# A second PSUM bank for the gates' matmuls, one bank fewer for the rest, and seven one-hot buffers in a one-core decoder block

## The chip, the cores and the metric

The kernel runs on one core of a Trainium2 chip. The metric is the device time of the program in microseconds (us). The core has engines that run side by side, each through its own queue in order: TensorE (PE, with its weight loads PEld), VectorE (DVE), ScalarE (ACT), GpSimd (POOL) and SyncE (SP, which here only issues transfers). The 16 DMA engines move the data. Matmuls write to PSUM, which has eight banks of 2 KiB per partition; ScalarE and VectorE empty it.

## What is computed

One decoder block on 1024 tokens of width 1024, in float32. Its first half is a mixer (sliding-window attention with sinks on 8 heads, and a short gated convolution, behind one input and before one output projection) with a residual and a layer norm. Its second half picks experts: for each token and each of 8 heads, 16 of 16384 single-neuron experts are chosen by two half keys, and their outputs are added up.

```python
h = layer_norm(DN_ALPHA * x + mix, ln1_g, ln1_b)
q = (h @ w_pq).reshape(T, 8, 256)
s1, s2 = q[..., :128] @ sub_keys1.T, q[..., 128:] @ sub_keys2.T
v1, i1 = top_k(s1, 16); v2, i2 = top_k(s2, 16)
cand = v1[..., :, None] + v2[..., None, :]
sc, pos = top_k(cand.reshape(T, 8, 256), 16)
e = i1[pos // 16] * 128 + i2[pos % 16];  g = softmax(sc)
a = gelu(einsum('tkd,td->tk', u_experts[e], h))
ff = einsum('tk,tkd->td', g * a, v_experts[e])
out = layer_norm(DN_ALPHA * h + ff, ln2_g, ln2_b)
```

## The kernel before

The tokens are eight blocks of 128. Three and a half of them (blocks 0, 6, 7 and half of block 1) are done by gathering rows: for each of the 128 chosen experts, GpSimd issues one indirect transfer that fetches a 1024-wide row of `u` (line 170) and later of `v` (line 183) for every token, and VectorE makes one pass over it (lines 172 and 185). The other four and a half blocks, 576 tokens, are done densely: every expert is computed for every token on TensorE, and a table of gates says which counts.

**Stage 1** (lines 211 to 683) goes through four groups of two blocks. For each group `project` multiplies 42 chunks of weights (line 399, eight matmuls a chunk): attention (`scores`, `values`), convolution (`conv`), output projection (`mixed`), norm (`normed`), and 16 chunks of expert queries with their key scores and searches (`keys_of`, lines 225 to 229 by `topk16`). While group g+1 is projected, a generator `side` works off what group g left: `product_keys` searches the candidates and decodes the chosen indices (lines 311 to 372), and for dense blocks `gates_of_all` builds the gate table. It takes eight tokens at a time: VectorE makes three one-hot tiles (`o1` in line 285, `oh` and `ol` in line 290; tag `hot`, four buffers for all three and for `f3`), TensorE multiplies them into a bank `pk` of four tokens (lines 296 and 297), and ScalarE empties the bank in two halves into the staging tiles `st` (line 300). After four such steps, one chunk of 32 tokens, SyncE stores both `st` tiles to the table `gd` in HBM (line 304); `st` has two buffers, so one set. There are 72 steps and 18 chunks. All other PSUM work of stage 1 uses `pm` (the projections, two banks) and `pt` (transposes, scores, the attention's `po`, all under the tag `tp`, three banks); the row passes hold two banks (`pg`). The gathered rows are put between the projections by `advance_rows`.

**Stage 2** (from line 686) reuses the SBUF space of stage 1. It loads the normed activations back (`hr`, split into `hT` on ScalarE and VectorE, lines 693 to 697), then runs 128 steps `up` (line 715) and 128 steps `down` (line 751) of 48 matmuls each, reading the gate table by `gq` (line 719). VectorE splits weights (`ul`, line 125), multiplies by gates (line 723), adds up (line 759), and makes the remaining row passes between.

What sets the order: the program is written in one stream, and a scheduler places its instructions engine by engine by its own timeline of the program, with the number of buffers and banks as limits. So a change of buffer counts can move instructions anywhere.

Of the kernel before, what the change touches and what calls it, by code (L numbers as in the profile page):

```python
# [13 lines left out]
F32 = mybir.dt.float32  # L14
F32R = mybir.dt.float32r
F16 = mybir.dt.float16
# [6 lines left out]
PS = bass.MemoryType.PSUM  # L23
DR = bass.MemoryType.DRAM

P = 128
# [27 lines left out]
OT = 8  # L54
# [25 lines left out]
def block_kernel(ctx: ExitStack, tc: tile.TileContext, d, out):  # L80
# [131 lines left out]
    with ExitStack() as s1:  # L212
        pa = s1.enter_context(tc.tile_pool(name="pa", bufs=1))
        gb = s1.enter_context(tc.tile_pool(name="gb", bufs=1))
        p1 = s1.enter_context(tc.tile_pool(name="p1", bufs=1))
        p2 = s1.enter_context(tc.tile_pool(name="p2", bufs=1))
        pk = s1.enter_context(tc.tile_pool(name="pk", bufs=1, space=PS))
        pm = s1.enter_context(tc.tile_pool(name="pm", bufs=2, space=PS))
        pt = s1.enter_context(tc.tile_pool(name="pt", bufs=3, space=PS))

        bias = p1.tile([P, 26], F32, name="bias")
        nc.sync.dma_start(bias, d["bias"])
# [14 lines left out]
        def gates_of_all(tb, e1, e2, g, first=0):  # L237


            f3 = gb.tile([P, 3, P], F32, name="f3", tag="hot", bufs=4)  # L240
            ei = gb.tile([P, P], I32, name="ei")
            V.tensor_copy(f3[:, 0], e1.rearrange("p h k -> p (h k)"))
            V.tensor_copy(ei, e2.rearrange("p h k -> p (h k)"))
            V.tensor_scalar(ei, ei, 7, None, op0=ALU.bitwise_and)
            V.tensor_copy(f3[:, 2], ei)
            V.tensor_tensor(f3[:, 1], e2.rearrange("p h k -> p (h k)"), f3[:, 2], op=ALU.subtract)
            tp = pk.tile([P, 4, P], F32, name="pk")
            for i in range(3):
                nc.tensor.transpose(tp[:, i], f3[:, i], ident)
            nc.tensor.transpose(tp[:, 3], g.rearrange("p h k -> p (h k)"), ident)  # L250
            iT = gb.tile([P, 5, P], F16, name="iT", bufs=2)
            act(iT[:, 0:3], tp[:, 0:3], AF.Copy)
            act(iT[:, 3], tp[:, 3], AF.Copy, scale=GSCALE)
            V.scalar_tensor_tensor(iT[:, 4], tp[:, 3], GSCALE, iT[:, 3], op0=ALU.mult, op1=ALU.subtract)
            i1w = gb.tile([P, P, OT], F16, name="i1w")
            act(i1w, tp[:, 0, :, None].to_broadcast([P, P, OT]), AF.Copy)

            def wide(o, i, n, step, t0):
                wshp = [P, n, HB // OT, OT]
                V.tensor_tensor(o.rearrange("p n (a t) -> p n a t", t=OT),  # L260
                                iT[:, i, t0:t0 + HB].rearrange("p (a t) -> p a t", t=OT)[:, None].to_broadcast(wshp),
                                keys[:, 0:n * step:step, None, :].to_broadcast(wshp), op=ALU.is_equal)

            shp = [P, P, OT]
            shr = [P, OT, P // OT, OT]
            for t0 in range(first, P, TG):
                if t0 % HB == 0:
                    da = gb.tile([P, 16, HB], F16, name="da")
                    wide(da, 1, 16, 8, t0)
                    db = gb.tile([P, 3, 8, HB], F16, name="db")  # L270
                    wide(db[:, 0], 2, 8, 1, t0)
                    for i in (1, 2):
                        V.tensor_tensor(db[:, i], db[:, 0], iT[:, 2 + i, None, t0:t0 + HB].to_broadcast([P, 8, HB]),
                                        op=ALU.mult)
                st = [gb.tile([P, NC // 2, TG], F32, name="st", bufs=2) for _ in range(2)]
                for t1 in range(t0, t0 + TG, OT):
                    ts = slice(t1, t1 + OT)
                    td = slice(t1 % HB, t1 % HB + OT)

                    def mk(name):  # L280
                        return gb.tile(shp, F16, name=name, tag="hot", bufs=4)

                    o1 = gb.tile([P, OT, P], F16, name="o1", tag="hot", bufs=4)
                    oh, ol = mk("oh"), mk("ol")
                    V.tensor_tensor(o1.rearrange("p t (a b) -> p t a b", b=OT),  # L285
                                    i1w[:, ts, None, :].to_broadcast(shr),
                                    row.rearrange("p (a b) -> p a b", b=OT)[:, None].to_broadcast(shr),
                                    op=ALU.is_equal)
                    for o, i in ((oh, 1), (ol, 2)):
                        V.tensor_tensor(o.rearrange("p (a b) t -> p a b t", b=8),  # L290
                                        da[:, :, None, td].to_broadcast([P, 16, 8, OT]),
                                        db[:, i, None, :, td].to_broadcast([P, 16, 8, OT]), op=ALU.mult)
                    for t2 in range(0, OT, 4):
                        ps = pk.tile([P, 4, P], F32, name="pk")
                        for t in range(4):
                            nc.tensor.matmul(ps[:, t], oh[:, :, t2 + t], o1[:, t2 + t], start=True, stop=False)  # L296
                            nc.tensor.matmul(ps[:, t], ol[:, :, t2 + t], o1[:, t2 + t], start=False, stop=True)
                        tt = t1 - t0 + t2
                        for z in range(2):
                            act(st[z][:, :, tt:tt + 4].rearrange("p n t -> p t n"),  # L300
                                ps[:, :, z * 64:(z + 1) * 64], AF.Copy, scale=1.0 / GSCALE)
                        yield
                for z in range(2):
                    nc.sync.dma_start(gd[(tb * P + t0 - DT0) // TG, :, z * 64:(z + 1) * 64], st[z])

        def product_keys(tb, v16, i16):
# [67 lines left out]
            if tb not in ROWS or tb == SHARED:  # L374
                yield from gates_of_all(tb, e1, e2, g, HALF if tb == SHARED else 0)
# [482 lines left out]
```

## Time and profile before

| | us |
|---|---|
| median of 3 runs | 2876.57 (2875.49 to 2882.86) |
| the profiled execution | 2877.42 |
| its span, first to last instruction | 2875.7 |
| TensorE busy | 2533.8 (88%) |
| VectorE busy | 2217.7 (77%) |
| GpSimd / ScalarE busy | 1286.0 / 845.0 |

Shares of busy time are means over both stages, which have different limits, so the stages are read apart: by slices, by stretches, and by what each engine waited for. The granted clock of TensorE has two levels here, 2.4 GHz (1.00 in the profile) and 1.2 GHz (0.50). Durations of neighbouring instructions can overlap a little, since one starts while the last one drains.

### The profile page before, as it was taken

The numbers are of one execution on the slowest core, as the hardware profiler recorded it, in microseconds if no ns is written. First come the engines' busy times: TensorE is split into PE (matmuls) and PEld (weight loads), VectorE is DVE, ScalarE is ACT, GpSimd is POOL, SyncE is SP. The second block draws the span as 40 slices with busy tenths as digits, with TensorE's granted clock in tenths as the row PEclk, the third lists the DMA queues.
The fourth block names the chain that finished last, engine by engine and source line by source line (L and its number), as shares of the span: only waits on it lengthen the run. The fifth ranks groups of instructions, "written<-read, shape, count | busy, mean of one in ns | idle before, by whom it ended". The sixth has DMA issues, their size and how long they took to land.

```text
span 2875.7 us, 45661 instructions
## 1 busy us (share of the span) xinstructions
PE 2533.8 (88%) x17220; PEld 2399.3 (83%) x17220; DVE 2217.7 (77%) x5055; ACT 845.0 (29%) x1486; POOL 1286.0 (45%) x1110
## 2 busy tenths in 40 slices
PE   9998899799868322199999999999999999999997
PEld 7887787678657222199999999999999999999997
DVE  2259999999999999678888888888888888632335
ACT  2213232232443333242222322232222222322322
POOL 0001533543433345356756666666666666312121
PEclk9899899799879555599999999999999999999998
DMA  6346999999888787989999999999999999633322
GB/s 206 98 157 213 358 359 343 335 345 328 302 309 304 264 303 269 333 273 360 335 331 347 337 334 329 333 337 342 334 331 334 332 331 337 232 115 104 108 88 74
DMA packets 285597, 805.36 MB, mean 280 GB/s; under 512 B 24992, under 2 KB 105152, under 8 KB 280640
## 3 DMA queue, kind: packets, MB, share of 16 engines
q0 software_dynamic: 132160, 481.39, 46.1%
q1 hardware_dynamic: 153216, 321.06, 32.8%
q8 instruction: 135, 2.21, 0.3%
q14 instruction: 86, 0.70, 0.1%
HBM read 753.56 MB, written 48.50 MB: 279 GB/s over the span
## 4 chain that ended last, share of the span: by engine, by line
PE 58%; DVE 12%; DMA 5%; issue 3%; POOL 1%; ACT 1%; POOLq 0%; DVEq 0%; ACTq 0%
PE pd L751 28%; PE pd L715 28%; DVE pg L185 2%; PE mm L399 2%; DVE row L172 2%; DMA row<-in_v,ix 2%; DMA gd<-st 1%; DMA row<-in_u,ix 1%; DVE ol L290 1%; DVE o L285 1%; DVE oh L290 1%; DMA uraw<-in_uT 1%; DVE scr L227 1%; ACT st L300 0%; DVE i L229 0%
## 5 line engine op out<-in xcount | busy, mean ns | idle before, releaser
L715 PE MATMUL pd<-hT,uh 128*128 128x288 f32 x4096 | 710.9, 296 | 46.6 <-ACT uh L124 46.6
L183 POOL DMA_INDIRECT row<-in_v,ix x448 | 495.2, 1105 | 487.9 <-DVE pg L185 240.5
L170 POOL DMA_INDIRECT row<-in_u,ix x448 | 462.6, 1032 | 542.7 <-DVE row L172 214.5
L715 PEld LDWEIGHTS pd<-hT,uh 128*128 128x128 f32 x4096 | 602.6, 189 | 46.8 <-ACT uh L124 46.8
L185 DVE SCALAR_TENSOR_TENSOR pg<-row,a,pg 128x1024 f32<-128x1024 f32 x448 | 574.2, 1282 | 29.9 <-DMA row<-in_v,ix 25.5
L172 DVE SCALAR_TENSOR_TENSOR row<-row,pg 128x1024 f32<-128x1024 f32 x448 | 536.3, 1213 | 30.3 <-DMA row<-in_u,ix 24.9
L125 POOL TENSOR_TENSOR vl<-vraw,vh 128x1024 fp32r<-128x1024 f32 x128 | 307.3, 2401 | 350.2 <-ACT vh L124 346.7
L751 PE MATMUL pd<-Wl,vh 128*128 128x288 f32 x2048 | 442.8, 295 | 0.0
L751 PE MATMUL pd<-Wh,vl 128*128 128x288 f32 x2048 | 442.3, 295 | 0.6 <-POOL vl L125 0.6
L751 PE MATMUL pd<-Wh,vh 128*128 128x288 f32 x2048 | 441.4, 295 | 0.7 <-DVE accT L759 0.7
L715 PE MATMUL pd<-hT,ul 128*128 128x288 f32 x2048 | 437.9, 295 | 0.0
L759 DVE TENSOR_TENSOR accT<-accT,pd 128x288 f32<-128x288 f32 x496 | 203.5, 450 | 216.5 <-PE pd L751 211.6
L751 PEld LDWEIGHTS pd<-Wh,vl 128*128 128x128 f32 x2048 | 330.9, 188 | 0.8 <-POOL vl L125 0.8
L751 PEld LDWEIGHTS pd<-Wh,vh 128*128 128x128 f32 x2048 | 330.5, 188 | 1.1 <-issue 0.9
L751 PEld LDWEIGHTS pd<-Wl,vh 128*128 128x128 f32 x2048 | 331.1, 188 | 0.1
L715 PEld LDWEIGHTS pd<-hT,ul 128*128 128x128 f32 x2048 | 329.8, 189 | 0.3 <-DVE ul L125 0.3
L124 ACT ACTIVATE vh<-vraw 128x1024 fp32r<-128x1024 f32 x128 | 135.8, 1061 | 537.1 <-PE pd L751 455.1
L125 DVE TENSOR_TENSOR ul<-uraw,uh 128x1024 fp32r<-128x1024 f32 x128 | 159.2, 1244 | 173.9 <-ACT uh L124 166.5
L296 PE MATMUL pk<-o,oh 128*128 128x128 f16 x576 | 116.7, 267 | 182.7 <-DVE oh L290 89.8
L399 PE MATMUL mm<-x,raw 128*128 128x256 f32 x1152 | 267.8, 384 | 7.9 <-DMA x<-in_xT 7.0
L399 PEld LDWEIGHTS mm<-x,raw 128*128 128x128 f32 x1152 | 213.6, 192 | 39.2 <-DMA raw<-in_wall 6.0
L124 ACT ACTIVATE uh<-uraw 128x1024 fp32r<-128x1024 f32 x128 | 135.8, 1061 | 370.4 <-PE pd L715 319.8
(218 smaller groups left out, 2977.5 us busy)
## 6 DMA issues: line engine op xcount, KB each, us to landing
raw<-in_wall SPq DMA_DIRECT2D x168, 512.0 KB
uraw<-in_uT SPq DMA_DIRECT2D x128, 512.0 KB
vraw<-in_vL SPq DMA_DIRECT2D x128, 512.0 KB
gd<-st SPq DMA_DIRECT2D x36, 1024.0 KB
gq<-gd SPq DMA_DIRECT2D x32, 1152.0 KB
row<-in_u,ix POOLq DMA_INDIRECT x448
row<-in_v,ix POOLq DMA_INDIRECT x448
x<-in_xT SPq DMA_DIRECT2D x16, 256.0 KB
```

The source lines that it names most:

```text
L124: act(dh, src, AF.Copy)
L125: eng.tensor_tensor(dl, src, dh.bitcast(F32), op=ALU.subtract)
L170: G.indirect_dma_start(out=row, out_offset=None, in_=d["u"], in_offset=bass.IndirectOffsetOnAxis(ap=ix[:, k:k + 1], axis=0))
L172: V.scalar_tensor_tensor(row, row, 1.0, h1p, op0=ALU.mult, op1=ALU.mult, accum_out=a[:, k:k + 1])
L183: G.indirect_dma_start(out=row, out_offset=None, in_=d["v"], in_offset=bass.IndirectOffsetOnAxis(ap=ix[:, k:k + 1], axis=0))
L185: V.scalar_tensor_tensor(acc, row, a[:, k:k + 1], acc, op0=ALU.mult, op1=ALU.add)
L290: V.tensor_tensor(o.rearrange("p (a b) t -> p a b t", b=8), da[:, :, None, td].to_broadcast([P, 16, 8, OT]), db[:, i, None, :, td].to_broa ...
L296: nc.tensor.matmul(ps[:, t], oh[:, :, t2 + t], o1[:, t2 + t], start=True, stop=False)
L399: nc.tensor.matmul(ps[:, :n], w[:, j], mov[:, j, :n], start=(j == 0), stop=(j == NJ - 1))
L715: nc.tensor.matmul(ps[i][:, :n], w[:, j], hT[z][:, j, offs[i]:offs[i] + n], start=(j == 0 and k == 0), stop=(j == NJ - 1 and k == 2))
L751: nc.tensor.matmul(ps[i][:, :n], vv[:, j % 2, k], w[:, offs[i]:offs[i] + n], start=(k == 0 and p == 0), stop=(k == QUAD - 1 and p == 2))
L759: V.tensor_tensor(o, o, ps[i][:, :n], op=ALU.add)
```

## The change

Three pools get other sizes; no line of the computation changes. The gates' pool `pk` goes from one PSUM bank to two, and the pool `pt` of all other transposes and scores from three to two (the sum stays eight banks). The tag `hot`, which the one-hot tiles and `f3` share, goes from four to seven buffers of 2 KiB per partition.

```diff
--- before.py
+++ after.py
@@ -214,9 +214,9 @@
         gb = s1.enter_context(tc.tile_pool(name="gb", bufs=1))
         p1 = s1.enter_context(tc.tile_pool(name="p1", bufs=1))
         p2 = s1.enter_context(tc.tile_pool(name="p2", bufs=1))
-        pk = s1.enter_context(tc.tile_pool(name="pk", bufs=1, space=PS))
+        pk = s1.enter_context(tc.tile_pool(name="pk", bufs=2, space=PS))
         pm = s1.enter_context(tc.tile_pool(name="pm", bufs=2, space=PS))
-        pt = s1.enter_context(tc.tile_pool(name="pt", bufs=3, space=PS))
+        pt = s1.enter_context(tc.tile_pool(name="pt", bufs=2, space=PS))
 
         bias = p1.tile([P, 26], F32, name="bias")
         nc.sync.dma_start(bias, d["bias"])
@@ -237,7 +237,7 @@
         def gates_of_all(tb, e1, e2, g, first=0):
 
 
-            f3 = gb.tile([P, 3, P], F32, name="f3", tag="hot", bufs=4)
+            f3 = gb.tile([P, 3, P], F32, name="f3", tag="hot", bufs=7)
             ei = gb.tile([P, P], I32, name="ei")
             V.tensor_copy(f3[:, 0], e1.rearrange("p h k -> p (h k)"))
             V.tensor_copy(ei, e2.rearrange("p h k -> p (h k)"))
@@ -278,9 +278,9 @@
                     td = slice(t1 % HB, t1 % HB + OT)
 
                     def mk(name):
-                        return gb.tile(shp, F16, name=name, tag="hot", bufs=4)
-
-                    o1 = gb.tile([P, OT, P], F16, name="o1", tag="hot", bufs=4)
+                        return gb.tile(shp, F16, name=name, tag="hot", bufs=7)
+
+                    o1 = gb.tile([P, OT, P], F16, name="o1", tag="hot", bufs=7)
                     oh, ol = mk("oh"), mk("ol")
                     V.tensor_tensor(o1.rearrange("p t (a b) -> p t a b", b=OT),
                                     i1w[:, ts, None, :].to_broadcast(shr),
```

The scheduler then finds another order. At three places, as its rows stand (an "x" with a number at a row's end says that it comes so often in a row):

SyncE, end of stage 1 before: `raw` are the weight loads, `gd` the stores of the gate table, `hr`, `gq` and `uraw` the first loads of stage 2.

```order
L563 DMA h1d<-r 128x1024 x2
L391 DMA raw<-in_wall 128x1024 x4
L304 DMA gd<-st 128x2048 x2
L391 DMA raw<-in_wall 128x1024 x7
L304 DMA gd<-st 128x2048 x18
L696 DMA hr<-hTd 128x1152 x4
L719 DMA gq<-gd 128x18x128 x2
L707 DMA uraw<-in_uT 128x1024 x5
```

The same place in the order of the changed kernel:

```order
L304 DMA gd<-st 128x2048 x6
L563 DMA h1d<-r 128x1024 x2
L391 DMA raw<-in_wall 128x1024
L304 DMA gd<-st 128x2048 x2
L391 DMA raw<-in_wall 128x1024 x8
L304 DMA gd<-st 128x2048 x2
L391 DMA raw<-in_wall 128x1024 x2
L304 DMA gd<-st 128x2048 x6
L696 DMA hr<-hTd 128x1152 x4
L719 DMA gq<-gd 128x18x128 x2
```

Half of the stores stood behind the last weight load; now a sixth of them do, and the gates run beside the projections.

VectorE, the change from stage 1 to stage 2 before: gathered rows of `v`, the last gate tiles, the decoding of the last blocks (`g`, `x`, `e`, `ix`), the split of `hT`, the first `ul`.

```order
L290 TENSOR_TENSOR oh<-da,db 128x1024
L290 TENSOR_TENSOR ol<-da,db 128x1024
L185 SCALAR_TENSOR_TENSOR pg<-row,a,pg 128x1024
L235 TENSOR_TENSOR e_9625<-x_9867 128x64
...
L235 TENSOR_TENSOR e_9626<-x_9868 128x64
L370 SCALAR_TENSOR_TENSOR ef<-e_9625,e_9626 128x128
L372 CAST ix_10118<-ef 128x128
L185 SCALAR_TENSOR_TENSOR pg<-row,a,pg 128x1024 x5
L125 TENSOR_TENSOR hT_8307<-hr,hT_8306 128x1152 x4
L185 SCALAR_TENSOR_TENSOR pg<-row,a,pg 128x1024 x5
L125 TENSOR_TENSOR ul<-uraw,uh 128x1024 x2
```

The same place in the changed kernel, where `v`, `i` and `tp` belong to the key scores of the last group:

```order
L290 TENSOR_TENSOR oh<-da,db 128x1024
L290 TENSOR_TENSOR ol<-da,db 128x1024
L172 SCALAR_TENSOR_TENSOR row,a<-row,pg 128x1024 x2
L228 MAX v_7305<-scr 128x8
L226 MAX_INDEX i_7308<-v_7306,tp 128x8
L227 MATCH_REPLACE scr<-v_7306,tp 128x128
...
L125 TENSOR_TENSOR hT_8307<-hr,hT_8306 128x1152
L228 MAX v_7306<-scr 128x8
L125 TENSOR_TENSOR hT_8307<-hr,hT_8306 128x1152
```

Before, the decoding of the last group was done when the split came, with 357 row passes ahead of it; now the key searches of that group are only just ending, its decoding follows in stage 2, and 297 row passes stand ahead.

TensorE, attention of group 0's second block before: `sp` are score banks, `S` the probabilities, `po` the output.

```order
L466 MATMUL sp_549<-maskb,identb 128x512
L472 MATMUL sp_549<-kT,qT 128x256 x2
L399 MATMUL mm<-x,raw 128x256 x8
L466 LDWEIGHTS identb
L466 MATMUL sp_550<-maskb,identb 128x512
L472 MATMUL sp_550<-kT,qT 128x256 x2
L500 MATMUL tp<-ident,S 128x128 x8
L507 MATMUL po<-vn,pT 128x64 x4
L500 MATMUL tp<-ident,S 128x128 x4
L507 MATMUL po<-vn,pT 128x64 x4
```

And in the changed kernel:

```order
L466 MATMUL sp_549<-maskb,identb 128x512
L472 MATMUL sp_549<-kT,qT 128x256 x2
L466 LDWEIGHTS identb
L466 MATMUL sp_550<-maskb,identb 128x512
L472 MATMUL sp_550<-kT,qT 128x256 x2
L500 MATMUL tp<-ident,S 128x128 x8
L507 MATMUL po<-vn,pT 128x64 x8
L500 MATMUL tp<-ident,S 128x128 x8
L507 MATMUL po<-vn,pT 128x64 x8
L514 MATMUL tp<-ident,ya 128x128 x4
```

The chunk of projection between the two score banks is gone from there (it stands earlier), and transposes and output matmuls alternate in eights instead of fours.

## Rows read from the trace of the kernel before

**Rows 1.** The page's 40 slices of 72 us: busy tenths; PEclk granted clock.

```profile
PE   9998899799868322199999999999999999999997
...
DVE  2259999999999999678888888888888888632335
...
PEclk9899899799879555599999999999999999999998
```

**Rows 2.** Busy time by stretch: its length, each engine (x instructions), clock, DMA share, GB/s.

```profile
0.00:216.00 216.00, 204.78 (x1003) 177.04 (x1004) 72.18 (x366) 47.31 (x120) 7.51 (x62) 0.96 0.47 154
216.00:936.00 720.00, 617.67 (x3398) 528.36 (x3398) 694.21 (x2303) 238.78 (x516) 273.53 (x264) 0.90 0.88 320
936.00:1168.00 232.00, 71.26 (x487) 55.35 (x486) 218.11 (x589) 81.27 (x143) 104.38 (x97) 0.50 0.79 277
...
1400.00:2440.00 1040.00, 1040.00 (x7838) 1040.00 (x7837) 871.88 (x1239) 286.33 (x419) 675.13 (x532) 1.00 0.94 335
2440.00:2860.00 420.00, 416.59 (x3133) 416.32 (x3132) 174.48 (x294) 115.99 (x171) 92.60 (x50) 1.00 0.39 123
```

**Rows 3.** Timeline, end of stage 1: start us, length us, what [idle before].

```profile
1165.20 0.69 DVE L290 TENSOR_TENSOR oh<-da,db 128x1024 f16<-128x1024 f16 x1
...
1170.48 1.29 DVE L185 SCALAR_TENSOR_TENSOR pg<-row,a,pg 128x1024 f32<-128x1024 f32 x1
...
1171.68 0.68 DVE L362 TENSOR_TENSOR g<-b,rnk 128x1024 f16<-128x1024 f16 x1
...
1193.13 5.16 DVE L125 TENSOR_TENSOR hT<-hr,hT 128x1152 fp32r<-128x1152 f32 x4
...
1197.75 20.05 SPq L707 DMA_DIRECT2D uraw<-in_uT  x5
...
1216.23 1.33 PE L715 MATMUL pd<-hT,uh 128*128 128x288 f32 x4 [46.58 <-ACT uh L124]
```

**Rows 4.** Waits, 0 to 1180 us: us in total, times, longest.

```profile
PE pk L296 <- DVE oh L290: 89.8, 25, 10.9
PE pk L296 <- ACT st L300: 85.9, 54, 8.5
```

**Rows 5.** VectorE by line, 216 to 1168 us: count, busy us, mean ns, idle before.

```profile
L172 DVE SCALAR_TENSOR_TENSOR row<-row,pg 128x1024 f32<-128x1024 f32 x192 | 230.5, 1210 | 19.3 <-DMA row<-in_u,ix 14.8 <-issue 4.3
L185 DVE SCALAR_TENSOR_TENSOR pg<-row,a,pg 128x1024 f32<-128x1024 f32 x155 | 198.0, 1277 | 3.0 <-DMA row<-in_v,ix 3.0
...
L290 DVE TENSOR_TENSOR oh<-da,db 128x1024 f16<-128x1024 f16 x72 | 49.0, 680 | 8.2 <-PE pk L296 7.0 <-issue 1.1
...
L225 DVE MAX8 v<-tp 128x8 f32<-128x128 f32 x100 | 28.6, 288 | 7.0 <-PE tp L589 7.0
...
L228 DVE MAX8 sc<-scr 128x8 f32<-128x50 f32 x64 | 13.2, 206 | 0.4
...
L232 DVE TENSOR_TENSOR x<-x 128x512 f16<-128x512 f16 x31 | 12.9, 416 | 0.0
...
L356 DVE TENSOR_TENSOR ge<-ge,dst 128x1024 f16<-128x1024 f16 x16 | 11.0, 689 | 0.0
...
L225 DVE MAX8 sc<-cand 128x8 f32<-128x50 f32 x64 | 9.0, 193 | 0.0
```

**Rows 6.** Timeline, attention of group 0's second block.

```profile
79.92 3.72 PE L399 MATMUL mm<-x,raw 128*128 128x256 f32 x16
...
91.44 0.60 ACT L501 ACTIVATE pT<-tp 128x512 f32<-128x512 f32 x1 [2.48 <-PE tp L500]
...
97.14 0.69 DVE L511 TENSOR_TENSOR ya<-po,den 128x512 f32<-128x512 f32 x1 [8.72 <-PE po L507]
```

**Rows 7.** The gates' eviction by line; two store pieces of the chain of work.

```profile
L300 ACT ACTIVATE st<-pk 128x256 f32<-128x256 f32 x288 | 154.2, 630 | 271.3 <-PE pk L297 177.8 <-DMA gd<-st 54.0 <-issue 23.6
...
796.83 10.37 DMA gd<-st
...
1087.43 11.84 DMA gd<-st
```


## The prediction

> **What bounds the kernel now.** I read the page's slices first [rows 1]. They show three parts. TensorE is nearly full until about 936 us, then almost idle with its clock at 0.5, and full again from about 1220 us to the end. VectorE is full from about 200 us to 1200 us. The table by stretch [rows 2] makes this exact. From 0 to 216 us TensorE is busy 204.8 of 216 us and VectorE 72.2: TensorE sets the pace. From 216 to 1168 us VectorE is busy 694.2 + 218.1 = 912.3 of 952 us, 95.8%: VectorE sets the pace, also in the last 232 us of it, where TensorE works 71.3 us and clock 0.50 is granted. From 1216 us on TensorE never stops (1040.0 of 1040), so stage 2 has a fixed length, 2875.7 - 1216.2 = 1659.5 us after its first matmul [rows 3]. What the change is worth is therefore read from one thing: how early that first matmul can start, and whether TensorE stays fed afterwards.
>
> The waits [rows 4] are of the kind that a second gate bank removes: the gates' matmuls waited 85.9 us for ScalarE to empty the single `pk` bank and 89.8 us for VectorE's one-hot tiles. But TensorE is not the bound there. VectorE, which is, waited only 7.0 us for a `hot` buffer, 7.0 us for key scores and some 18 us for gathered rows [rows 5].
>
> **Part by part.** *(1) The bank and the buffers themselves.* On VectorE they can give back the 7.0 us of the `oh` row [rows 5] and no more. A statement that speaks against more is in the Trainium skill, "TensorE: Matmul & The Clock Gate", section "HAM oscillation — how this bites in real kernels": in its kernel, adding PSUM double-buffering on top of the loop fix gave no further gain. By that alone the sum would be 2877.4 - 7 = 2870.
>
> *(2) The order.* The larger effect is that the scheduler, given a gate path that no longer blocks, places the gates earlier. In the order of SyncE 18 of the 36 gate stores stand behind the last weight load before and 6 after. On VectorE, 357 gathered-row instructions stand ahead of the first `hT` split before and 297 after, so 60 rows (23 of line 172, 37 of line 185) and most of the decoding of the last two token blocks move behind the start of stage 2. Their price, from the durations in [rows 5]: 23 x 1.20 (230.5/192) = 27.6; 37 x 1.28 = 47.3; 16 heads x 5 searches of about 0.20 (0.193 to 0.206) = 16; four half blocks of decoding, each five wide operations of 0.689 and three add trees of about 1.1 (the first step 0.416, the later ones shorter), 4 x 6.7 = 27; and some 45 small operations, about 10. That is 128 us of rows. Rows overlap: in [rows 3] a 1.29 us instruction is followed by the next after 1.20, so about 0.09 us of each of the 250 is not the engine's time, 23 us. It leaves 105 us of VectorE, and at 95.8% busy 105/0.958 = **110 us** that the split of `hT` comes earlier. What lies between the last gate and the first matmul, 1216.2 - 1165.2 = 51 us of stores, the `hTd` load, the split and the first `uraw` load [rows 3], stays: the same steps stand there in the same order in both programs, with key searches in the gaps.
>
> Can TensorE keep up? From 216 to 1168 us it was busy 617.7 + 71.3 us [rows 2], the second at half clock, so some 655 us at full clock, against 842 us in the shorter stretch. It has room (78%), so VectorE stays the bound if the two don't get in each other's way.
>
> *(3) Two general banks instead of three (`pt`).* In the first 216 us TensorE is the bound and this costs directly. The attention of the second block loses a chunk of projection that stood between its score matmuls (3.72 us in [rows 6]), and with `po` holding one of two banks the transposes of the probabilities wait for each eviction of 0.60 us instead of running beside it, four times per block; TensorE and VectorE already wait on that chain (8.72 us ahead of `ya`, [rows 6]). At the low end it all hides under projections that the scheduler moved there (0); at the high end both blocks of group 0 pay 3.7 + 4 x 0.9, about 15. I take +8. In the later groups it lands on TensorE's slack.
>
> *(4) The gates packed closer.* A 32-token chunk is 16 evictions of 0.535 us (154.2/288) and then a store that took 10.4 and 11.8 us before the two staging tiles were free again [rows 7]; `st` still has one set. So a chunk can't pass faster than 8.6 + 11 = 19 to 20 us or so. Before, the order left 22 us or more of VectorE work per chunk everywhere; after, eight of the 18 chunks have only 11 to 19 us (by the durations above), so VectorE reaches an `oh` tile whose buffer is still held, and all behind it on VectorE waits, rows and key searches too; ScalarE, in order, holds the projections' evictions back meanwhile. Bounds: -7 (the old `oh` wait goes and nothing comes) to +54 (ScalarE's waits for the store in [rows 7], all turned into VectorE's). Seven buffers let VectorE run some two steps ahead, so I take +20, nearer to the eight chunks x 2 to 3 us than to the upper end.
>
> *(5) The start of stage 2* now carries the decoding (some 100 operations in the first twelve `up` steps) while each group of four `up` and four `down` is 51 us of TensorE. Before, VectorE was busy 871.9 of 1040 us there [rows 2], 8 us free per group; the new order carries some 28 us more VectorE work in the first five groups, four and a half times 51 us long, which offer about 36 us. The sum is about even: 0 to +15, I take +3. Later the density is the same 22 rows per group in both orders and the rows only last three groups longer; from 2440 to 2860 us VectorE was busy 174.5 of 420 us and the DMA engines 0.39 [rows 2], so the 60 rows x 1.28 = 77 us have a cover. If that were gone, they would come back in full.
>
> *Sum:* -110 + 8 + 20 + 3 = -79. The profiled execution took 2877.4 us (span 2875.7), 0.9 above the median of the three runs, which is 2876.6: **2798 us**.
>
> **Rivals.** *Nothing new gets in the way:* VectorE stays at 96% with the buffers' help, (3) hides and (4) gives: 2877.4 - 110 - 7 = 2760. For it: an order made by the same scheduler reached 96% before. Against: the store, which the order takes to be shorter than the 10 us and more it took.
>
> *Only the direct effect*, the rule of (1) carried through: the moved work comes back in stage 2, because its DMA engines are at 0.94 [rows 2] and 60 more rows can't be fetched while the expert blocks stream. Price: as (2) is returned, 2870. For: 0.94. Against: the rows' density is not raised, only their end moves from about 2440 us into a stretch at 0.39. The page's own result fits the waits seen (they were not on the bound), but not the order.
>
> *Slower: two general banks starve VectorE.* Key scores of a chunk sit in a `tp` bank until VectorE has searched them, ten searches of 0.288 us [rows 5], 2.9 us for the chunk's two blocks. If in the three VectorE-bound groups each of 48 chunks makes VectorE wait one such turn, because TensorE couldn't run ahead, that is 139 us: 2877.4 - 110 + 139 + 8 = 2914. It decides from 110 us of added waits on, 13% of the stretch. For: TensorE and VectorE now finish stage 1 together, with little lead. Against: with three banks VectorE waited only 7.0 us for scores after 216 us [rows 5], and two banks still let one chunk be computed while another is searched.
>
> *The order changes nothing on the chip* (the moved rows were free time before) is excluded by 95.8%.
>
> **How the numbers follow.** Forecast, with its own range of 2775 to 2830: 0.62. Nothing in the way, 2760: 0.22. Direct effect only, 2870: 0.07. Slower, 2914: 0.09. The likeliest is 2798. The range goes down to 2877.4 - 110 - 7 - 3, about 2757, and up by the bounds to 2877.4 - 110 + 15 + 54 + 15 = 2851, which leaves out the last two cases, 0.16. A measurement here tells 0.3% (9 us) from no change; faster than 2868 are the first two cases and a little of the third: 0.86; within 0.3%: 0.05; slower: 0.09.
>
> **What would show it.** In the profile after: the first matmul of line 715 near 1135 us, with 1660 us behind it (steps 2 and 5); no stretch of 230 us with TensorE at clock 0.50, but gates among the projections; VectorE's busy share between 216 us and the last gate at 92 to 94%, the lost part standing ahead of `oh` with `pk` or the store as cause (4), or ahead of key scores (slower rival); the last projection-free attention chain of group 0 longer by some 4 us (3). It is wrong if the first matmul comes at 1135 us but TensorE then waits (direct effect only), if it comes before 1105 us, or if VectorE's share falls under 85%.

## The result and the profile after

| | before | after |
|---|---|---|
| median of 3 runs, us | 2876.57 (2875.49 to 2882.86) | 2772.84 (2772.08 to 2774.97) |
| span of the profiled execution | 2875.7 | 2771.1 |
| VectorE busy in the span | 2217.7 (77%) | 2230.0 (80%) |
| last one-hot tile `oh` of the gates starts | 1165.2 | 1049.4 |
| first matmul of stage 2 starts | 1216.2 | 1095.1 |
| from there to the end of the span | 1659.5 | 1676.0 |

The ratio is 0.9635, with a 95% interval of 0.9612 to 0.9658: 104 us faster. The forecast was 2798, its range 2757 to 2851.

The slices of after, to be laid beside [rows 1]; one slice is 69 us:

```profile
PE   8899699798687673999999999999999999999997
...
DVE  2158889999999999999688788888888888886335
...
PEclk9899699789887685999999999999999999999998
```

The hole in TensorE's row (2 2 1 before) has shrunk to one slice. The same by stretch, as in [rows 2] (length, TensorE, weight loads, VectorE, ScalarE, GpSimd, each with its instructions, then clock, DMA share, GB/s):

```profile
0.00:216.00 216.00, 201.06 (x966) 171.79 (x967) 67.74 (x339) 46.86 (x118) 7.50 (x62) 0.94 0.45 150
216.00:936.00 720.00, 584.20 (x3284) 497.28 (x3282) 688.51 (x2191) 244.88 (x537) 293.81 (x258) 0.86 0.87 314
936.00:1049.00 113.00, 91.39 (x594) 80.89 (x595) 106.56 (x314) 45.57 (x96) 43.52 (x41) 0.88 0.91 329
1095.00:1117.00 22.00, 19.63 (x124) 19.29 (x125) 21.62 (x84) 8.89 (x13) 9.39 (x7) 0.78 0.80 290
1117.00:1300.00 183.00, 177.60 (x1314) 176.20 (x1314) 178.63 (x285) 63.51 (x101) 124.50 (x86) 0.99 0.88 301
1300.00:2340.00 1040.00, 1037.30 (x7798) 1036.71 (x7797) 861.98 (x1290) 291.56 (x425) 668.80 (x532) 1.00 0.94 333
```

Three things are to be read here. VectorE is still the busy engine of stage 1: from 216 to 1049 us 688.5 + 106.6 = 795.1 of 833 us, 95.4%, against 95.8% before. It simply has 114 us less to do there (909.3 us before the last `oh` of before). The stretch from 936 us to the last gate, 229 us at clock 0.50 in before, is 113 us at 0.88: gates now stand among projections. And at the start of stage 2 VectorE is full (178.6 of 183 us), which it wasn't before. Here are the 83 us that begin 22 us behind the first matmul of stage 2, before and after:

```profile
1238.00:1321.00 83.00, 82.27 (x616) 81.86 (x615) 62.36 (x79) 35.20 (x60) 48.75 (x39) 1.00 0.88 306
```

```profile
1117.00:1200.00 83.00, 78.35 (x574) 77.41 (x573) 81.06 (x156) 36.82 (x61) 53.49 (x36) 0.98 0.87 291
```

The gates' waits, TensorE's from 0 to 1060 us (beside [rows 4]) and VectorE's from 216 to 1050 us (us in total, times, longest):

```profile
PE pk L296 <- ACT st L300: 32.7, 41, 6.1
...
PE pk L296 <- DVE oh L290: 16.5, 5, 6.7
```

```profile
DVE row L172 <- DMA row<-in_u,ix: 11.2, 14, 2.5
DVE v L225 <- PE tp L589: 11.1, 8, 5.0
DVE oh L290 <- PE pk L296: 4.7, 3, 2.5
```

TensorE's two waits fell from 85.9 and 89.8 us to 32.7 and 16.5. VectorE still waits little. That alone doesn't say whether fewer waits made VectorE's list shorter, or whether the list only came to be ordered in another way. The experiments take these apart.

### The profile page after: what moved, and what is told of

It is laid out like the page before. It is cut to its first block, busy times and chain, and to the rows that moved or that the text cites. A ratio compares the mean times of both kernels' runs of the same rounds, so it can differ in the third digit from the quotient of the medians.

```text
span 2771.1 us, 45703 instructions
## 1 busy us (share of the span) xinstructions
PE 2532.0 (91%) x17220; PEld 2401.0 (87%) x17220; DVE 2230.0 (80%) x5055; ACT 832.0 (30%) x1485; POOL 1320.7 (48%) x1110
## 4 chain that ended last, share of the span: by engine, by line
PE 60%; DVE 13%; DMA 4%; ACT 3%; issue 2%; POOL 0%; ACTq 0%; DVEq 0%; POOLq 0%
PE pd L751 27%; PE pd L715 26%; PE mm L399 6%; DVE row L172 3%; DMA gd<-st 2%; ACT st L300 2%; DVE pg L185 1%; DMA row<-in_u,ix 1%; PE pk L296 1%; DVE scr L227 1%; PE pk L297 1%; DVE ul L125 0%; DVE oh L290 0%; DVE nm L476 0%; DVE o L285 0%
## 5 line engine op out<-in xcount | busy, mean ns | idle before, releaser
L183 POOL DMA_INDIRECT row<-in_v,ix x448 | 531.4, 1186 | 434.3 <-DVE pg L185 209.0
L399 PE MATMUL mm<-h,raw 128*128 128x256 f32 x1024 | 236.7, 385 | 1.3 <-ACT h L568 0.7
L124 ACT ACTIVATE uh<-uraw 128x1024 fp32r<-128x1024 f32 x128 | 135.7, 1060 | 338.3 <-PE pd L715 329.7
```

Of the source, the lines that this page charges most:

```text
L124: act(dh, src, AF.Copy)
L183: G.indirect_dma_start(out=row, out_offset=None, in_=d["v"], in_offset=bass.IndirectOffsetOnAxis(ap=ix[:, k:k + 1], axis=0))
L399: nc.tensor.matmul(ps[:, :n], w[:, j], mov[:, j, :n], start=(j == 0), stop=(j == NJ - 1))
```

## The experiments

Two explanations stood against each other. **Theory A:** the amount of work that the order puts on VectorE ahead of the last gate sets the end of stage 1; the buffer sizes act through the order alone. **Theory B:** the gates' own chain (fill the bank, empty it, store a chunk) sets it, and row passes are filler in VectorE's idle time, so that only the bank and the tiles matter.

All runs in one table. "Work" is VectorE's busy time from 216 us to the start of the last `oh`, "idle" is the rest of that stretch, "`oh` wait" the part of it that stood ahead of an `oh` tile with `pk` as its cause; the last two columns are the first matmul of stage 2 and the time from it to the end of the span. The times in the second column are medians; all columns behind it are of the profiled execution, which lay 10 us above the median in e1, 5 in e3 and at most 3 in the others. The median of before itself lay between 2876.6 and 2879.6 us in the sessions, so 3 us between two rows say nothing.

| kernel | us | work | idle | `oh` wait | 1st matmul | after it |
|---|---|---|---|---|---|---|
| before | 2876.6 | 909.3 | 39.7 | 7.0 | 1216.2 | 1659.5 |
| after | 2772.8 | 795.1 | 38.3 | 4.7 | 1095.1 | 1676.0 |
| e1 `pt` 2 alone | 2896.0 | 924.2 | 45.8 | 9.2 | 1236.7 | 1667.6 |
| e2 seven tiles alone | 2793.1 | 820.3 | 51.7 | 15.0 | 1135.1 | 1654.4 |
| e3 second bank alone | 2811.3 | 854.6 | 44.4 | 9.2 | 1158.5 | 1656.5 |
| e4 before, 285 rows | 2836.6 | 845.2 | 66.2 | 35.1 | 1178.0 | 1653.8 |
| e5 before, after's load | 2830.5 | 804.0 | 98.0 | 63.9 | 1166.2 | 1661.8 |
| e6 seven tiles, same load | 2794.1 | 805.3 | 66.7 | 27.4 | 1136.9 | 1657.3 |
| e7 second bank, same load | 2789.2 | 809.5 | 54.5 | 22.4 | 1121.5 | 1668.3 |
| e8 after, 240 rows | 2734.4 | 764.5 | 47.5 | 12.2 | 1068.7 | 1664.7 |
| e9 e5 with TensorE's order pinned | 2843.7 | 806.8 | 113.3 | 43.4 | 1184.3 | 1655.2 |
| e10 before, TensorE's order pinned | 2882.3 | 899.6 | 57.4 | 18.5 | 1216.1 | 1661.4 |
| e11 after, 200 rows | 2720.4 | 712.0 | 77.0 | 26.7 | 1048.5 | 1672.6 |
| e12 e11, search paced | 2721.1 | 710.4 | 77.1 | 27.7 | 1052.0 | 1670.4 |

### One edit at a time (e1 to e3)

```diff
# e1
-        pt = s1.enter_context(tc.tile_pool(name="pt", bufs=3, space=PS))
+        pt = s1.enter_context(tc.tile_pool(name="pt", bufs=2, space=PS))
# e2 (the same in all three places)
-            f3 = gb.tile([P, 3, P], F32, name="f3", tag="hot", bufs=4)
+            f3 = gb.tile([P, 3, P], F32, name="f3", tag="hot", bufs=7)
# e3: the edit of e1, and
-        pk = s1.enter_context(tc.tile_pool(name="pk", bufs=1, space=PS))
+        pk = s1.enter_context(tc.tile_pool(name="pk", bufs=2, space=PS))
```

> Before with one edit: the pool pt has 2 buffers instead of 3; pk keeps its one bank and the one-hot tiles their four, so a PSUM bank lies idle. This prices step (3) by itself. In the program's order 358 row passes stand ahead of the last gate tile on VectorE (345 in before). Theory A (VectorE's work ahead of the last gate sets the end of stage 1, and a row pass there costs some 1.25 us): 13 passes more are 13 x 1.25 / 0.95 = 17 us, and the attention of the first blocks some 6 us later as in the profile of after: about 2900 us, 2885 to 2910. Theory B (the chain of the gates through one PSUM bank, its evictions and its stores sets the end of stage 1, and rows only fill VectorE's idle time): the rows add nothing, 2880 to 2885 us from the attention alone.

Measured: 2896.01 us, ratio 1.0069 (1.0043 to 1.0095). As A said. The attention of the first group shows the price of giving up the third general bank; the row of e1 that answers to `ya` in [rows 6], and after's:

```profile
103.55 0.69 DVE L511 TENSOR_TENSOR ya<-po,den 128x512 f32<-128x512 f32 x1 [10.14 <-PE po L507]
```

```profile
103.32 0.69 DVE L511 TENSOR_TENSOR ya<-po,den 128x512 f32<-128x512 f32 x1 [10.14 <-PE po L507]
```

Some 6 us later than before's 97.14 in both. The first matmul of stage 2 comes 20.5 us later in e1: 15 us more work that the order put on VectorE, and 6 us more idle time. The further 8 us behind that matmul are those of a profiled execution 10 us above the median.

> Before with one edit: seven buffers for the one-hot tiles instead of four; one PSUM bank for the gates and three for pt as in before. In the order 294 row passes stand ahead of the last gate tile (345 in before). Theory A: 51 passes fewer are 51 x 1.25 / 0.95 = 67 us less ahead of stage 2, less some 15 us that the start of stage 2 gives back as in after: about 2825 us, 2800 to 2840. Theory B: one bank still holds the chain of the gates, and the time stays near before, 2860 to 2880 us.

Measured: 2793.06 us, ratio 0.9721 (0.9694 to 0.9748): better than either theory said. The tiles alone give four fifths of the gain.

> After without its last edit: two banks for the gates and two buffers for pt, but four one-hot tiles as in before. In the order 320 row passes stand ahead of the last gate tile (345 in before, 285 in after). Theory A: 25 passes fewer are 25 x 1.25 / 0.95 = 33 us, the attention takes back 6 and the start of stage 2 some 5: about 2855 us, 2840 to 2865. Theory B: the second bank is what shortens the chain of the gates, so that nearly all of the gain is there without the buffers: 2775 to 2800 us.

Measured: 2811.3 us, ratio 0.9768 (0.974 to 0.9796), between the two. In all three the last gate follows the work on VectorE: e2 and e3 have 89 and 55 us less of it than before and reach the first matmul 81 and 58 us earlier. My count of the rows alone had left out that the search and part of the decoding of the last blocks moved too. So far A; but in e2 and e3 order and buffers still change together.

### The load of after on the buffers of before (e4, e5)

```diff
+    def row_pass(*args, **kw):
+        passes[0] += 1
+        if passes[0] > 285 and gates:            # gates: the ol tiles (line 290) so far
+            with tc.issue_after(gates[-1].ins):  # stands behind it in VectorE's order
+                V.scalar_tensor_tensor(*args, **kw)
+        else:
+            V.scalar_tensor_tensor(*args, **kw)
# e5 also: every VectorE instruction of product_keys of blocks 6 and 7 stands behind it
```

> Before with its buffers untouched; the row passes from the 286th on are made to stand behind the last gate tile in VectorE's order, so that 285 stand ahead of it, as many as in after (345 in before). The decoding of the last group stays ahead of it. Theory A: 60 passes fewer are 60 x 1.25 / 0.95 = 79 us less ahead of stage 2, less 5 to 20 us at its start: about 2810 us, 2795 to 2820, most of what after gains without either of its edits. Theory B: with one bank and four tiles the gates go on at their own pace, VectorE merely stands idle more: 2860 to 2880 us.

Measured: 2836.61 us, ratio 0.9869 (0.9843 to 0.9895). Neither: 43 us, not 70, and not none.

> Before with its buffers untouched, and VectorE's order ahead of the last gate tile cut to that of after: 285 row passes ahead of it, and the candidate search and the decoding of blocks 6 and 7 held behind it (in e4 only the rows were held). Theory A (the amount of work on VectorE ahead of the last gate sets the end of stage 1, the buffers act through the order alone): as after, 2775 to 2790 us. Theory B (the chain of the gates through one bank has its own pace): VectorE stands idle in the tail instead, as it did in e4 for 42 of 191 us, and the time is that of e4, 2825 to 2840 us.

Measured: 2830.45 us, ratio 0.9836 (0.9819 to 0.9852). VectorE has 105 us less to do than in before, but only 47 us come of it; the other 58 are idle time that wasn't there. VectorE's waits in e5, from 216 to 1118 us:

```profile
DVE oh L313 <- PE pk L320: 63.9, 20, 9.5
DVE row L165 <- DMA row<-in_u,ix: 12.0, 13, 2.1
```

The timeline of e5 shows the wait (start us, length us, what, idle before it and what ended that):

```profile
1020.22 0.69 DVE L313 TENSOR_TENSOR oh<-da,db 128x1024 f16<-128x1024 f16 x1 [9.46 <-PE pk L320]
...
1021.43 0.26 PE L320 MATMUL pk<-o,oh 128*128 128x128 f16 x1 [1.14 <-ACT st L324]
...
1022.58 1.02 ACT L324 ACTIVATE st<-pk 128x256 f32<-128x256 f32 x2 [1.20 <-PE pk L321]
...
1023.65 0.26 PE L320 MATMUL pk<-o,oh 128*128 128x128 f16 x1 [1.11 <-ACT st L324]
...
1024.59 0.69 DVE L313 TENSOR_TENSOR oh<-da,db 128x1024 f16<-128x1024 f16 x1 [2.47 <-PE pk L320]
...
1028.97 0.69 DVE L313 TENSOR_TENSOR oh<-da,db 128x1024 f16<-128x1024 f16 x1 [2.48 <-PE pk L320]
```

TensorE and ScalarE take turns on the one bank: some eight matmuls, two evictions, eight matmuls, two evictions, and the next `oh` comes 4.37 us after the last. After every fourth step the store of the chunk stands in the way too: ahead of the 9.46 us ScalarE had waited 7.1 and 3.1 us for the staging tiles. The stretch from 936 us to the last gate, with the columns of [rows 2]:

```profile
936.00:1118.00 182.00, 66.41 (x472) 53.74 (x472) 108.19 (x261) 65.92 (x123) 35.15 (x34) 0.50 0.48 179
```

That is 29 steps in 182 us, 6.3 us a step, with VectorE busy only 108.2 us; 63.1 of the 63.9 us of `oh` waits lie in this stretch. So theory A fails as the only cause: at this load the chain of the gates is the bound. The store is a part of that chain, with 35.7 us of ScalarE's waits here; `st` has one set in every kernel, and what a second set would give no run shows.

### One buffer at a time, at the same load (e6, e7)

```diff
# e6: e5 with the edit of e2
# e7: e5 with the edits of e3
```

> As e5, with seven one-hot tiles and still one bank for the gates. Theory A: as after, 2775 to 2790 us. Theory B, if the bank is the limit: no better than hot7 as the scheduler orders it (2793), 2790 to 2815 us, with VectorE idle on PE pk in the tail; if the tiles were the limit: 2775 us.

Measured: 2794.06 us, ratio 0.9699 (0.9679 to 0.9718).

> As e5, with two banks for the gates, two buffers for pt and four one-hot tiles: after without its seven tiles, but with after's amount of work on VectorE ahead of the last gate. Theory A: as after, 2770 to 2785 us, so that the seven tiles act through the order alone. Theory B, if four tiles hold VectorE back: above 2795 us, with VectorE idle on PE pk ahead of the gate tiles.

Measured: 2789.19 us, ratio 0.9686 (0.967 to 0.9702).

The work on VectorE is nearly equal in e5, e6, e7 (804 to 810 us), the time isn't: 2830, 2794, 2789, and 2773 in after (whose own order has some 10 us less work ahead, since a part of the key searches also lies behind). The differences to e5 are 36, 41 and 58 us, and the `oh` wait of 63.9 us falls by 36.5, 41.5 and 59.2. That they agree so closely is in part luck. Up to the last `oh` e6 gains 30 us and e7 38, since other waits grew in e6 and the work is 5 us more in e7; after gains 68.5, with 9 us less work, and gives 14 back in stage 2. But the `oh` wait is by far the largest of these terms in each. What each buffer takes away shows in TensorE's waits, in e6 from 216 to 1088 us and in e7 from 216 to 1080 us:

```profile
PE pk L320 <- ACT st L324: 104.6, 69, 10.6
PE pk L320 <- DVE oh L313: 7.0, 3, 5.9
```

```profile
PE pk L320 <- DVE oh L313: 31.5, 17, 9.6
PE pk L320 <- ACT st L324: 18.8, 15, 4.8
```

In e5 they are 90.5 (`st`) and 44.0 (`oh`). Seven tiles let VectorE finish one-hot tiles ahead, so TensorE no longer waits for them, but the bank is as busy as ever; the second bank takes the wait for the eviction. Either makes VectorE's wait short, and together they all but remove it. So theory B also fails as the only cause, but it holds at this load, and both edits do something there. The order of TensorE still changes with the buffers in these kernels, and the next two runs change it alone.

### The order of TensorE (e9, e10)

In TensorE's order 31.5 of the 72 gate steps stand behind the last projection in before and in e5, 19 with seven tiles, 16 with two banks and only 3 in after, which looks like a cause of its own, theory C.

```diff
# e9: as e5 (lag 8); e10: before, nothing held on VectorE (lag 32)
+            pinned = tc.issue_after(gate_mm[-1 - lag].ins) if gi == 3 and len(gate_mm) > lag else ExitStack()
+            with pinned:      # first matmul of a projection of the last group
+                nc.tensor.matmul(ps[:, :n], w[:, 0], mov[:, 0, :n], start=True, stop=False)
```

> The order of TensorE shows what theories A and B left out: of the 72 gate steps (eight tokens each) 31.5 stand behind the last projection matmul in before, 19 with seven tiles, 16 with two banks, 3 in after; in e5, for all its lighter VectorE, still 31.5. Theory C: those steps are a tail in which TensorE has nothing else to do, and with one bank a step there takes 6.3 us at the least (e5: 182 us for 29 steps, VectorE idle 74 of them). This kernel has before's one bank and four tiles, VectorE's load ahead of the last gate tile as in e5, and the first matmul of each projection of the last group is put behind the gate steps traced up to eight quarter-steps before it, so that 5 steps are left behind the last projection. Theory C: 2775 to 2795 us, as after, without either of its edits. Theory B (one bank keeps its pace wherever the gates stand, so that TensorE now waits in between): 2825 us or more, as e5.

Measured: 2843.68 us, ratio 0.9888 (0.9858 to 0.9918), 13 us more than e5. Theory C falls as a cause that would do without the buffers.

> Before with its buffers and its amount of work on VectorE (346 row passes ahead of the last gate tile, 345 in before; nothing else held); only TensorE's order is pinned as in e9, with 32 quarter-steps of slack, so that 17 gate steps are left behind the last projection instead of 31.5. Theory A (the amount of work on VectorE alone): no gain, 2865 to 2885 us. Theory C in its strong form (the tail alone): 14.5 steps fewer at 6.3 us are 91 us less, 2785 to 2800 us. If both limits stand side by side, VectorE being busy over 94 per cent of the tail already: nearer to A.

Measured: 2882.3 us, ratio 1.0016 (1.0003 to 1.0029): no gain, as A said at before's full load. VectorE's waits in e9, from 216 to 1136 us, say why interleaving alone doesn't help:

```profile
DVE oh L315 <- PE pk L322: 40.9, 20, 7.9
DVE r L584 <- PE tp L581: 22.1, 5, 5.5
DVE v L248 <- PE tp L619: 16.6, 9, 3.9
```

With one more wait of 2.5 us ahead of the last tile that is 43.4 us, 20.5 less than in e5. But TensorE, in order, now holds up projections, transposes and key scores while it waits for its one bank (82.4 us on `st`, in e5 90.5), and VectorE waits for those: `r` and `v`, 38.7 us, of which e5 has 7.3. In after the same interleaving meets a wait of only some 30 us on `st`, with the second bank and the tiles. So the order of TensorE alone gives nothing on the old buffers. Whether the buffers would give as much with the gates left in a tail no run shows: in e6, e7 and after they come with an order that moves gates forward.

### Further down the same road (e8, e11, e12)

```diff
# e8: after, with the row_pass of e4 and 240 in place of 285
# e11: 200
# e12: e11, and product_keys of blocks 6 and 7 behind the newest Wl split of line 724
```

> After with the row passes from the 241st on made to stand behind the last gate tile in VectorE's order: 240 ahead of it, where after has 285. Theory A: 45 passes fewer are 45 x 1.25 / 0.95 = 59 us less, until TensorE, which is busy 676 of the 834 us from 216 to 1050 us, is the next to be late; less 5 to 10 us at the start of stage 2: about 2720 us, 2710 to 2740, faster than both kernels. Theory B: VectorE's share of 95 per cent is filler, taking rows away leaves it idle: 2760 to 2775 us.

Measured: 2734.38 us, ratio 0.9502 (0.9486 to 0.9519). As A said, though not by its sum: VectorE's work falls by 30.6 us, not by 45 x 1.25, because search and decoding moved into the free places, and the time falls by 38.

> As e8, with 200 row passes ahead of the last gate tile instead of 240 (after: 285). Theory A: e8 lost 30 us of VectorE's work ahead of the last gate tile for 45 rows, since search and decoding moved in, and gained 38 us; here 40 rows go and 25 searches too, 55 us of work: 2680 us. Theory C (5 steps behind the last projection instead of 9, 5.4 us each, the rest bounded by TensorE's own work): 20 us less, 2705 to 2720 us. If the rows that are put off no longer fit under the second stage: above 2734 us.

Measured: 2720.35 us, ratio 0.9454 (0.9422 to 0.9485). The fastest kernel of the study, 52 us under after, with e12. Theory A's 2680 is missed, and C's range is met at its upper end. VectorE's work fell by another 52.5 us and the time by 14: the idle time grew from 47.5 to 77.0 us, of which the `oh` waits make 14.5 (12.2 to 26.7). Here the gates' chain begins to hold VectorE up again, with two banks now.

> As e11 (200 row passes ahead of the last gate tile; 2720.35 us), and the candidate search and the decoding of blocks 6 and 7 are made to stand behind the splits of the units that the second stage has reached, some 20 portions over its first ten ups, instead of wherever VectorE is free. It tests step (5): the second stage takes 1659.5 us in before and 1676.0 in after, and after's windows show VectorE at 98 to 100 per cent from 1117 to 1260 us while TensorE, full in before, loses 9 us of work and 7 of clock. Theory (VectorE's backlog of held-over search and decoding delays the splits that TensorE waits for): the second stage, 1672.6 us in e11, comes back to 1660 to 1665, the whole to 2705 to 2713 us. Rival (the loss has another cause, the rows' transfers or a cold clock): no change, 2717 to 2724 us. If the rows of block 6 come too late through it: above 2725.

Measured: 2721.14 us, ratio 0.9456 (0.9443 to 0.9469): no change. What TensorE waited for in stage 2 changed only its name. The waits of e11 from 1049 us and of e12 from 1052 us to the end (the first line of each lies ahead of the first matmul):

```profile
PE pd L727 <- ACT uh L124: 38.6, 1, 38.6
PE pd L727 <- DVE ul L125: 8.6, 3, 5.6
PE pd L763 <- DVE accT L771: 0.4, 1, 0.4
```

```profile
PE pd L747 <- ACT uh L139: 44.0, 1, 44.0
PE pd L783 <- DVE accT L791: 13.1, 5, 4.6
```

The splits `ul` are no longer late, but the additions to `accT` are: the same work, spread over ten steps, still fills VectorE there. TensorE's loss moved with it. In e11 TensorE was busy 16.4 of the first 22 us; in e12 it was full for the first 82 us (1052 to 1134) and lost 3.3 of the next 20, in which VectorE was busy all 20. That VectorE's backlog delays stage 2 is in agreement with this and with both lists, but e12 was meant to show it by a gain and didn't; it stays likely, not shown.

## Why the prediction was right, and where it was off

**What bounds stage 1: right, at the load of before.** VectorE at 95.8% was the bound; e10 shows that another order on TensorE with the same work on VectorE gains nothing, and e1, with 15 us more work on it, reaches stage 2 20.5 us later.

**(1) The bank and the buffers themselves, at most 7 us: wrong in size.** The working priced them by VectorE's wait in before (7.0 us), that is at before's load. The order that comes with them lowers that load by 105 to 114 us, and there the same buffers, with the order of TensorE that comes with them, are worth up to 58 us: 2830.5 (e5) against 2772.8, some 9 us of which are less work in after. Beside it stood a statement of the Trainium skill, "TensorE: Matmul & The Clock Gate", section "HAM oscillation — how this bites in real kernels": in its kernel PSUM double-buffering gave no further gain. It doesn't carry over to e7 against e5, where the second bank is worth 41 us; how it would be at before's load no run here shows.

**(2) The order, 110 us: right in size, half of it for a reason not named.** The last gate came 115.8 us earlier and VectorE had 114 us less work ahead of it. But e5, with nearly the same rows, search and decoding behind the last gate (804 us of work ahead of it) and the old buffers, gains only 47. Moving the work pays only as far as the gates' chain can follow. The 51 us from the last gate to the first matmul, which were to stay, became 45.7.

**(3) Two general banks, +8: near.** `ya` came 6.2 us later in after and 6.4 in e1; what of it reaches the end of stage 1 wasn't measured by itself.

**(4) The gates packed closer, +20: the term that failed.** ScalarE's wait for the store, put down in [rows 7] as the thing that would become VectorE's, did grow, to 67.6 us in 21 waits, but it stayed on ScalarE: VectorE's share was 95.4%, not 92 to 94, and its `oh` wait 4.7 us to the last gate. ScalarE's waits from 216 to 1050 us in after:

```profile
ACT st L300 <- DMA gd<-st: 67.6, 21, 8.7
```

The mechanism is real (e5's 63.9 us are that give-back and more), but at this load it belongs to one bank and four tiles. I had charged it to the kernel that has the buffers against it, at 20 us, and to the buffers I had credited nothing.

**(5) The start of stage 2, +3: too small.** It was +16.5 us. In the first 305 us after its first matmul TensorE was busy 294.5 us in after and 303.5 in before, which is 9.0. The rest fits the lower granted clock of those stretches, between the levels of 1.2 and 2.4 GHz: 0.78 against 0.90 in the first 22 us, 0.91 for 20 us and 0.97 for 100 us where before has 1.00, an estimate of 22 x 0.12 + 20 x 0.09 + 100 x 0.03, some 7 us. The estimate spread 28 us of extra work over five groups of steps; the order put search, decoding and rows into the first 165 us, in which VectorE was busy 162.7. That this is the cause of the loss is likely, not shown (e12).

**The sum.** -110 + 8 + 20 + 3 = -79 was forecast; -121 for the first matmul and +16.5 behind it, -105, was measured. By its own test, the first matmul ahead of 1105 us, the stage-1 half of the forecast was wrong: 1095.1. The measured 2772.8 lies in the whole range, but 2 us under the 2775 to 2830 of the likeliest case, and nearer to the rival "nothing in the way" (2760) than to 2798. Neither case is quite what happened: nothing got in the way in stage 1, which ended 39 us earlier than forecast, and stage 2 took back 16.5 us instead of 3. So two misses of opposite sign partly cancelled, and that the total came within 25 us is in part luck. The slower rival's wait, VectorE for key scores in two `tp` banks, is there at 11.1 us (7.0 before), not 139.

## What to carry to other kernels

A busy share of 96% that a scheduler has filled up is both a bound and a choice: look for work on that engine which isn't due yet, and pin it behind the stage's last critical instruction (here worth 43 us for 60 row passes on the old buffers, and 38 and then 14 us for 45 and 40 more on the new ones). Price a buffer at the load that the kernel will have after the change, not at the load before it, since a wait of 7 us can be 64 us once the filler is gone. When an edit changes buffers and order at once, run each on the other's: the new order on the old buffers told more here than undoing either edit.

## What the runs showed that was not expected

From 936 us to the last gate the one-bank chain had the same pace with four tiles and with seven: 6.3 us a step in e5 (29 steps in 182 us) and 6.3 in e6 (24 in 152). Where projections were pinned between the gates, in e9, it was 7.7 (26 in 200). With two banks it was 5.8 in e7 (25 in 144) and 5.4 in e8 (17 in 92, beside projections), but 6.3 in after (18 in 113), where VectorE had less room.

The granted clock was 0.50 (1.2 GHz) from 936 us to the last gate in before and e5, where it was busy 70 of 229 and 66.4 of 182 us, and 0.88 over the same stretch in after, where gates and projections share the stretch (91.4 of 113 us). In e6 and e7 it was 0.61 and 0.73. So the clock changed along with the buffers, and no run takes the two apart. An estimate from the traces bounds it: the gates' own matmuls took 63.0 us in the 29 steps of e5, 2.2 a step, and 25.5 us in the 18 of after, 1.4 a step. At 1.4 the tail of e5 would be at most 22 us shorter, where VectorE waited 63.1. And in e9 one bank and four tiles were no faster than in e5, though the clock from 936 us to the last gate was 0.82.
